# Attention heads in pairs on two tiles of TensorE, and a decay product with constant left sides

## The chip, the cores and the metric

The program runs on one core of one Trainium2 chip. The metric is the device time of one execution in microseconds (us); three runs of the kernel before took 1456.83 to 1459.18 us, with a median of 1458.25. Profiles are of one execution each, so a time read from a row is from that execution. Engine names: PE is TensorE (PEld its weight loads), DVE is VectorE, ACT is ScalarE, POOL is GpSimd, SP the engine that issues the loads here.

## The reference, cut to what matters

Two layers over 256 tokens of width 1024. Each layer has a mixer (attention, a short convolution and a gated recurrence, HGRN, side by side, from one input projection and into one output projection) and a channel mixer (dense SwiGLU in the first layer, eight experts with two chosen per token in the second). The change lies in the attention: 8 heads of 64, queries in two blocks of 128, logits shifted by the cumulated log of a forget gate.

```python
dcum = jnp.cumsum(jax.nn.log_sigmoid(f_logit.astype(jnp.float32)), axis=1)
...
logits = (jnp.einsum('bhqd,bhkd->bhqk', q_i, k_t) * scale
          + d_i[..., None] - d_k[:, :, None, :])
mask = k_pos[None, :] <= q_pos[:, None]
p = jax.nn.softmax(jnp.where(mask, logits, MASK_VALUE), axis=-1)
return jnp.einsum('bhqk,bhkd->bhqd', p, v_t)
```

A constant that is added to a whole row of logits (the term `d_i`) does not change its softmax.

## The kernel before

**Layout.** Activations stand transposed: features on the 128 partitions, the 256 tokens in the free dimension. Weights come in float32 in 1 MB pieces (`Stream`, lines 46 to 133): SP loads a piece into a `raw` buffer or into a large block `b0` to `b3` that has come free, ACT rounds it to a high part `whi` (line 107), DVE takes the rest as a low part `wlo` (line 117), and each projection is three matmuls: high x high, high x low, low x high. These have the output tile `z`, all in `mm` (line 362), and are most of what PE does.

**Order.** The tile framework schedules: it takes the order of the program text as a priority and writes out for each engine one fixed order of instructions, with waits between engines. On the chip every engine goes through its list in that order. The list `self.bg` holds pieces of background work; `tick` (line 165) issues the next one or more of them between groups of projection matmuls, so attention stands amid the projection of the convolution's inputs (`cxb`, `cc`, lines 685 and 689), and the output projection follows (`project`, line 714).

**Attention** (lines 456 to 684). `forget` (line 463) cumulates the gate on 104 partitions, four copies of eight heads at partitions 0, 32, 64 and 96, and splits it into a rounded and a remaining part: `dd` and `frhs`. `scores(n)` (line 629) makes a left side `lh` for head n on DVE (two columns of `h1`, `h2` select the head's rows), and then, for each of the two query blocks `t`, three matmuls into one PSUM bank of the tag `S`: `lh` x `frhs` (104 rows, 256 columns) gives the difference of the decays, `qn` x `kn` (64 rows, those of an even or an odd head; float32, which PE does in two passes) adds the logits, and `identb` x `causal` adds the mask. `attend(n)` (line 644) takes the maximum (DVE, line 651), the exponential with its sum (ACT, line 652), scales by the reciprocal (DVE, lines 653 and 655), turns three blocks of 128 x 128 on PE (line 659), copies them out (ACT, line 661, `pT`), multiplies by the values `av` into the even or odd half of a bank's partitions and copies that to `ya` (line 665). The background alternates `attend(n)` and `scores(n + 2)`. `hgrn_out` (line 561) and `out_norm` (line 572, tiles `on`, `E`, `rr`, `B`) stand between them. `over(i)` (line 671) hands a block to the stream of weights, in the second mixer for the experts. PSUM banks: three with the tag `z`, two `lv`, three `S` (line 151).

Of the kernel before, what the change touches and what calls it, by code (L numbers as in the profile page):

```python
# [18 lines left out]
T = 256  # L19
KT = D // P  # L20
# [19 lines left out]
SM_FB = 76  # L40
# [95 lines left out]
class Kern:  # L136
# [20 lines left out]

    def bank(self, tag="S"):

# [19 lines left out]
        parts.pop(0)()  # L179
        self.st.between = parts  # L180

    def constants(self, scr, itb):
# [3 lines left out]
        jp, it, ith = scr[:, 0:P], scr[:, P:2 * P].rearrange("p (k c) -> p k c", k=KT), scr[:104, 256:264]  # L186
# [13 lines left out]
        def later():  # L200
# [20 lines left out]
            for i in range(2):  # L221
                t = m.tile([48, T], F32R, name=f"rr{i}")
# [5 lines left out]
            nc.gpsimd.iota(ith, pattern=[[1, 8]], base=0, channel_multiplier=-1)  # L228
            self.h1 = m.tile([104, 8], F32, name="h1")
            self.h2 = m.tile([104, 8], F32, name="h2")  # L230
            self.ra = m.tile([104, 1], F32, name="ra")
            self.rb = m.tile([104, 1], F32, name="rb")
            for t in (self.h1, self.h2, self.ra, self.rb):
                nc.vector.memset(t, 0.0)
            for o in (0, 32, 64, 96):
                nc.vector.tensor_scalar((self.h2 if o < 64 else self.h1)[o:o + 8], ith[o:o + 8], float(-o), None,
                                        ALU.is_equal)
            nc.vector.memset(self.ra[0:8], -1.0)
            for o in (64, 96):
                nc.vector.memset(self.rb[o:o + 8], 1.0)  # L240
            self.ones104 = m.tile([104, T], F32, name="ones104")
            nc.gpsimd.memset(self.ones104, 1.0)

            self.reset = m.tile([P, 2, P], F32, name="reset")
            nc.gpsimd.memset(self.reset, 1.0)
# [3 lines left out]
            for w in (1, 2, 4, 8, 16, 32, 64):  # L249
                n = 64 // w  # L250
# [15 lines left out]
            sm = lbt[:, 2:4]  # L266
# [131 lines left out]
    def mixer_body(self, l, plan, h, hk, next_col, ta, tl, to, sml):  # L398
        nc = self.nc
# [7 lines left out]
        late = [self.constants(b2[:, 6 * T:8 * T], b3[0:16, 0:4 * T])] if l == 0 else []  # L407


        def forget_weights():  # L410
            wf = self.sm[:, SM_WF + 64 * l:SM_WF + 64 * (l + 1)].rearrange("p (k h) -> p k h", h=8)
            nc.gpsimd.memset(wp.bitcast(F32), 0.0)
            nc.gpsimd.memset(wq.bitcast(F32), 0.0)
            for o in (0, 32, 64, 96):
# [5 lines left out]
        R = rt = R2 = None  # L420
# [35 lines left out]
        dd = sml.tile([104, T], F32R, name="dd", bufs=1)  # L456
        rhs = sml.tile([104, T], F32R, name="frhs", bufs=1)
        fx = ta.tile([104, T], F32, name="fx", tag="t2")
        fa = ta.tile([104, T], F32, name="fa", tag="t2")
        fb = self.sm[:104, SM_FB + l:SM_FB + l + 1]  # L460
        nc.vector.tensor_tensor(fx, pf[:104], R[:104], ALU.mult)

        def forget():
            nc.scalar.activation(fa, fx, AF.Abs, bias=fb)
            nc.scalar.activation(fa, fa, AF.Exp, scale=-1.0)
            nc.scalar.activation(fa, fa, AF.Ln, bias=1.0)
            nc.vector.tensor_scalar(fx, fx, fb, 0.0, ALU.add, ALU.min)
            nc.vector.tensor_tensor(fx, fx, fa, ALU.subtract)


            nc.vector.tensor_tensor_scan(fa, self.ones104, fx, 0.0, ALU.mult, ALU.add)
            nc.scalar.activation(dd, fa, AF.Copy)
            nc.vector.tensor_scalar(rhs, dd.bitcast(F32), self.ra, self.rb, ALU.mult, ALU.add)
            nc.vector.tensor_tensor(rhs[32:40], dd[32:40].bitcast(F32), fa[32:40], ALU.subtract)
            nc.vector.tensor_tensor(dd[96:104], fa[96:104], dd[96:104].bitcast(F32), ALU.subtract)


        cum = part(b2, 4, 2)
# [117 lines left out]
        av = part(b3, 4, 4).rearrange("p (t a) c -> p t (a c)", t=2)  # L596
# [27 lines left out]


        ya = part(b3, 0, 4)
        S = {}

        def scores(n):
            if n > 7:  # L630
                return
            r, c = even_odd[n % 2], n // 2
            lh = sml.tile([104, T], F32R, name="lh", bufs=2)
            nc.vector.tensor_scalar(lh, dd.bitcast(F32), self.h1[:, n:n + 1], self.h2[:, n:n + 1], ALU.mult, ALU.add)
            b = self.bank()
            S[n] = (b[:, T:T + P], b[:, 0:T])
            for t in (1, 0):
                w = (t + 1) * P

                self.mm(b[:, (1 - t) * T:(2 - t) * T], lh[:, toks[t]], rhs, True, False)  # L640
                self.mm(S[n][t], qn[r, c, toks[t]], kn[r, c, 0:w], False, False)
                self.mm(S[n][t][:, w - P:w], self.identb, self.causal, False, True)

        def attend(n):
            r, c, vs = even_odd[n % 2], n // 2, slice(n * 64, n * 64 + 64)
            Pm = sml.tile([P, 3, P], F32, name="Pm", bufs=2)
            pm = (Pm[:, 2], Pm[:, 0:2].rearrange("p a b -> p (a b)"))
            nm = sml.tile([P, 2], F32, name="nm")
            sm = sml.tile([P, 2], F32, name="ssum")
            for t in (1, 0):  # L650
                nc.vector.tensor_reduce(nm[:, t:t + 1], S[n][t], AX.X, ALU.max, negate=True)
                nc.scalar.activation(pm[t], S[n][t], AF.Exp, bias=nm[:, t:t + 1], accum_out=sm[:, t:t + 1])
            nc.vector.reciprocal(sm, sm)
            for t in (1, 0):
                nc.vector.tensor_scalar(pm[t], pm[t], sm[:, t:t + 1], None, ALU.mult)

            pt = self.bank()
            for i, b in enumerate((2, 0, 1)):
                nc.tensor.transpose(pt[:, i * P:(i + 1) * P], Pm[:, b], self.ident)  # L659
            pT = sml.tile([P, 3 * P], F32, name="pT", bufs=2)  # L660
            nc.scalar.activation(pT, pt[:, 0:3 * P], AF.Copy)
            o = self.bank()[r, :T]
            self.mm(o, av[:, 0, vs], pT[:, 0:T], True, False)
            self.mm(o[:, P:T], av[:, 1, vs], pT[:, T:3 * P], False, True)
            nc.scalar.activation(ya[r, c], o, AF.Copy)

        scores(0)
        scores(1)


        def over(i):
# [1 line left out]
            if next_col is None:  # L673
                self.st.more(lambda: self.block(i))

        for n in range(8):
            self.bg += [lambda n=n: attend(n), lambda n=n: scores(n + 2)]
            if n == 1:
# [3 lines left out]
            if n == 5:  # L682
                self.bg.append(lambda: over(0))
        self.tick(2)
        z = self.chunk_t(plan["cxb"], h, 4, 3)
# [710 lines left out]
def layout(inputs):  # L1396

    import numpy as np
    g = {n: np.asarray(a) for n, a in inputs.items()}
    arrays = {n: np.ascontiguousarray(g[n]) for n in _WEIGHTS}  # L1400
    arrays["xt"] = np.ascontiguousarray(g["x"][0].T)

    def cols(a):
        return a.reshape(-1, a.shape[-1] // P, P).transpose(2, 0, 1).reshape(P, -1)

    def rows(a):
        return a.reshape(-1, KT, P, 8).transpose(2, 0, 1, 3).reshape(P, -1)

    fb = np.zeros((P, 2), g["attn_f_bias"].dtype)
    for o in (0, 32, 64, 96):  # L1410
# [24 lines left out]
```

## Time and profile before

| what | value |
|---|---|
| median of three runs | 1458.25 us (1456.83 to 1459.18) |
| profiled execution | 1458.15 us, span 1456.4 us |
| busy, share of the span | PE 97%, DVE 84%, ACT 71%, POOL 1% |
| mean granted clock | 0.992 |
| HBM read | 433.20 MB, 298 GB/s over the span |

The span is from the first to the last instruction; about 1.8 us of the execution lie around it. Matmuls are pipelined: a row's duration includes the time in which the next one already runs, so costs on PE are read from start to start, not from durations, and a busy PE is not one at its peak. A timeline row with x2 or x16 merges so many instructions that follow each other; its first number is the start of the first. The chain of work goes back from the last instruction to whatever released each step, so it names the engine that others wait for.

### The profile page before, as it was taken

The numbers are of one execution on the slowest core, as the hardware profiler recorded it, in microseconds if no ns is written. First come the engines' busy times: TensorE is split into PE (matmuls) and PEld (weight loads), VectorE is DVE, ScalarE is ACT, GpSimd is POOL, SyncE is SP. The second block draws the span as 40 slices with busy tenths as digits, with TensorE's granted clock in tenths as the row PEclk, the third lists the DMA queues.
The fourth block names the chain that finished last, engine by engine and source line by source line (L and its number), as shares of the span: only waits on it lengthen the run. The fifth ranks groups of instructions, "written<-read, shape, count | busy, mean of one in ns | idle before, by whom it ended". The sixth has DMA issues, their size and how long they took to land.

```text
span 1456.4 us, 21819 instructions
## 1 busy us (share of the span) xinstructions
PE 1415.0 (97%) x8339; PEld 1210.2 (83%) x8339; DVE 1229.3 (84%) x1257; ACT 1034.3 (71%) x1072; POOL 18.7 (1%) x39
## 2 busy tenths in 40 slices
PE   7999999999999998999999999999999999999997
PEld 7887999999999786788888778878888788877875
DVE  8957865555588677799989999998999999999997
ACT  8546643443474555789878788988888888888884
POOL 4000000000000000000000000000000000000000
PEclk9999999999999998999999999999999999999999
DMA  8332555555552356799999999999999999999994
GB/s 284 110 102 88 174 174 183 194 174 190 187 174 88 116 177 211 281 381 407 411 404 378 384 390 411 411 413 402 395 413 411 403 405 411 412 413 411 412 411 173
DMA packets 186766, 435.73 MB, mean 299 GB/s; under 512 B 6816, under 2 KB 11040, under 8 KB 186656
## 3 DMA queue, kind: packets, MB, share of 16 engines
q1 hardware_dynamic: 186656, 434.28, 79.3%
q8 instruction: 67, 1.10, 0.3%
q14 instruction: 43, 0.35, 0.1%
HBM read 433.20 MB, written 1.05 MB: 298 GB/s over the span
## 4 chain that ended last, share of the span: by engine, by line
PE 83%; DVE 8%; DMA 3%; issue 2%; ACT 2%; DVEq 0%; ACTq 0%
PE z L362 50%; PE S L362 14%; PE lv L362 10%; PE ls L362 7%; DVE wlo L117 5%; DMA b<-moe_w_gate 2%; DMA raw<-moe_w_up 1%; ACT whi L107 1%; PE S L1005 1%; DVE y L1042 1%; DVE xT L1051 0%; PE S L659 0%; DVE on L540 0%; DMA raw<-moe_w_down 0%; DVE b L556 0%
## 5 line engine op out<-in xcount | busy, mean ns | idle before, releaser
L117 DVE TENSOR_TENSOR wlo<-raw,whi 128x1024 fp32r<-128x1024 f32 (+2 forms) x287 | 479.3, 1683 | 95.7 <-issue 50.2
L107 ACT ACTIVATE whi<-raw 128x1024 fp32r<-128x1024 f32 (+2 forms) x287 | 405.1, 1427 | 164.3 <-PE z L362 93.0
L117 DVE TENSOR_TENSOR wlo<-b,whi 128x2048 fp32r<-128x2048 f32 (+1 forms) x177 | 395.4, 2247 | 11.4 <-PE z L362 4.0
L362 PE MATMUL z<-whi,x 128*128 128x512 f32 x1232 | 367.7, 402 | 3.2 <-DVE x L934 2.6
L107 ACT ACTIVATE whi<-b 128x2048 fp32r<-128x2048 f32 (+1 forms) x177 | 332.9, 1884 | 32.8 <-PE lv L362 7.5
L362 PE MATMUL z<-wlo,x 128*128 128x512 f32 x896 | 283.9, 398 | 3.5 <-DVE wlo L117 3.2
L362 PEld LDWEIGHTS z<-whi,x 128*128 128x128 f32 x1232 | 225.5, 190 | 50.3 <-DVE x L934 3.1
L362 PE MATMUL z<-hi,whi 128*128 128x256 f32 x864 | 246.5, 286 | 7.4 <-ACT whi L107 7.0
L362 PE MATMUL z<-lo,whi 128*128 128x256 f32 x864 | 245.6, 285 | 0.0
L362 PE MATMUL z<-hi,wlo 128*128 128x256 f32 x864 | 245.5, 285 | 0.0
L362 PEld LDWEIGHTS z<-wlo,x 128*128 128x128 f32 x896 | 167.9, 189 | 49.1 <-DVE wlo L117 9.1
L362 PEld LDWEIGHTS z<-hi,whi 128*128 128x128 f32 x864 | 164.2, 190 | 10.9 <-ACT whi L107 7.0
L362 PEld LDWEIGHTS z<-lo,whi 128*128 128x128 f32 x864 | 164.3, 190 | 1.6 <-issue 1.3
L362 PEld LDWEIGHTS z<-hi,wlo 128*128 128x128 f32 x864 | 163.9, 190 | 2.1 <-issue 0.8
L362 PE MATMUL ls<-whi,ah 128*128 128x512 f32 x264 | 83.8, 396 | 0.0
L362 PE MATMUL ls<-wlo,ah 128*128 128x512 f32 x264 | 83.7, 396 | 0.0
L362 PEld LDWEIGHTS ls<-wlo,ah 128*128 128x128 f32 x264 | 49.5, 188 | 12.2 <-DVE wlo L117 0.3
L362 PEld LDWEIGHTS ls<-whi,ah 128*128 128x128 f32 x264 | 49.3, 188 | 11.6
L117 DVE TENSOR_TENSOR wlo<-x,whi 128x2048 fp32r<-128x2048 f32 x24 | 54.6, 2284 | 3.7 <-PE z L362 3.4
L362 PE MATMUL lv<-whi,al 128*128 128x512 f32 x168 | 53.2, 395 | 0.0
L362 PE MATMUL lv<-wlo,ah 128*128 128x512 f32 x168 | 53.2, 395 | 0.0
L362 PE MATMUL lv<-whi,ah 128*128 128x512 f32 x168 | 53.2, 395 | 0.0
(336 smaller groups left out, 1765.8 us busy)
## 6 DMA issues: line engine op xcount, KB each, us to landing
b<-moe_w_gate SPq DMA_DIRECT2D x59, 1024.0 KB, 9.4
b<-moe_w_up SPq DMA_DIRECT2D x57, 1024.0 KB, 10.2
b<-moe_w_down SPq DMA_DIRECT2D x56, 1024.0 KB, 9.8
raw<-moe_w_up SPq DMA_DIRECT2D x45, 1024.0 KB, 10.2
raw<-moe_w_down SPq DMA_DIRECT2D x43, 1024.0 KB, 9.7
raw<-moe_w_gate SPq DMA_DIRECT2D x42, 1024.0 KB, 9.7
raw<-w_in SPq DMA_DIRECT2D x22, 1024.0 KB, 4.9
raw<-ffn_w_gate SPq DMA_DIRECT2D x14, 1024.0 KB, 5.0
```

The source lines that it names most:

```text
L107: self.nc.scalar.activation(hi, x, AF.Copy)
L117: self.nc.vector.tensor_tensor(lo, x, self.hi[i][:, h * a:(h + 1) * a].bitcast(F32), ALU.subtract)
L362: self.nc.tensor.matmul(out, lhsT, rhs, start=start, stop=stop, skip_group_check=True)
L1005: nc.tensor.transpose(pt[:, q * P:(q + 1) * P], a[0][:, q * P:(q + 1) * P], self.ident)
L1042: nc.vector.scalar_tensor_tensor(y2[:, 1, c], y[c], gs[:, 0:1], y2[:, 0, c].bitcast(F32), ALU.mult, ALU.subtract)
```

## The change

Heads are taken in pairs, an even one on partitions 0 to 63 and an odd one on 64 to 127.

- The decay product: `head`, a constant of 72 x 8 x 128 written once, selects a head's row (0 to 7: rounded part, 64 to 71: remaining part) for all 128 queries. `frhs` has 384 columns, minus the cumulated gate of all 256 tokens and again of the first 128, so one matmul per head serves both query blocks. The term `d_i` is left out. `dd`, `lh`, `h1`, `h2`, `ra` and `rb` go.
- `scores(p)`: both heads' decay products, then the four query-key products with the heads in turn (two row tiles, two banks), then the four masks; PE's order within this block is the written one.
- `attend(n)` becomes three pieces of background work: `soft(p)` (maximum to scaling, for two heads), `turn(p)` (six transposes, the second head's into a bank `lv`, two copies), and `attend(p)` (values of both heads into the two halves of one bank `lv`, heads in turn, one copy for both). Per pair the background is `soft(p)`, `scores(p + 1)`, `turn(p)`, `attend(p)`; before the first, only `scores(0)` is issued.

```diff
-        def scores(n):
-            if n > 7:
+        S, pms, pTs = {}, {}, {}
+
+        def scores(p):
+            if p > 3:
                 return
...
+            b = [self.bank(), self.bank()]
+            S[p] = [(x[:, T:T + P], x[:, 0:T]) for x in b]
+            with self.tc.manual_schedule(engines={mybir.EngineType.PE}):
+                for u in range(2):
+                    self.mm(b[u][:, 0:3 * P], self.head[:, 2 * p + u], rhs, True, False)
+                for t in (1, 0):
+                    for u, r in enumerate(even_odd):
+                        self.mm(S[p][u][t], qn[r, p, toks[t]], kn[r, p, 0:(t + 1) * P], False, False)
             for t in (1, 0):
...
+                for u in range(2):
+                    self.mm(S[p][u][t][:, t * P:(t + 1) * P], self.identb, self.causal, False, True)
...
+        def turn(p):
+
+            pTs[p] = sml.tile([P, 2, 3 * P], F32, name="pT", bufs=2)
+            for u in range(2):
+                pt = self.bank("lv" if u else "S")
+                for i, b in enumerate((2, 0, 1)):
+                    nc.tensor.transpose(pt[:, i * P:(i + 1) * P], pms[p][:, u, b], self.ident)
+                nc.scalar.activation(pTs[p][:, u], pt[:, 0:3 * P], AF.Copy)
+
+        def attend(p):
+            o = self.bank("lv")[:, :T]
+            for k in range(2):
+                for u, r in enumerate(even_odd):
+                    vs = slice((2 * p + u) * 64, (2 * p + u + 1) * 64)
+                    self.mm(o[r, k * P:T], av[:, k, vs], pTs[p][:, u, k * T:k * P + T], k == 0, k == 1)
+            nc.scalar.activation(ya[:, p], o, AF.Copy)
...
+            nc.gpsimd.iota(ith, pattern=[[1, 8], [0, P]], base=0, channel_multiplier=-1)
+            self.head = m.tile([72, 8, P], F32R, name="head")
+            for p, o in ((slice(0, 64), 0), (slice(64, 72), 64)):
+                nc.vector.tensor_scalar(self.head[p].rearrange("p n q -> p (n q)"),
+                                        ith[p].rearrange("p n q -> p (n q)"), float(-o), None, ALU.is_equal)
...
+            nc.vector.tensor_tensor_scan(fa, self.ones72, fx, 0.0, ALU.mult, ALU.add)
+            nc.scalar.activation(rhs[:, 0:T], fa, AF.Copy, scale=-1.0)
+            lo = rhs[64:72, 0:T]
+            nc.vector.scalar_tensor_tensor(lo, fa[64:72], -1.0, lo.bitcast(F32), ALU.mult, ALU.subtract)
+            nc.scalar.activation(rhs[:, T:3 * P], rhs[:, 0:P].bitcast(F32), AF.Copy)
...
+        for p in range(4):
+            self.bg += [lambda p=p, f=f: f(p) for f in (soft, lambda p: scores(p + 1), turn, attend)]
+            if p == 0:
                 self.bg.append(hgrn_out)
-            if n == 3:
+            if p == 1:
                 self.bg += [lambda: out_norm(6, yr), lambda: out_norm(0, ya[:, 0:2]), lambda: over(1)]
```

How the change moves instructions shows in the orders of the built programs. PE in the first mixer, before: the end of head 0's scores and the beginning of head 1's (each `S_` with its number is a bank's tile, `b0_686` holds queries and keys).

```order
L362 MATMUL S_1060<-b0_686 128x128
L362 LDWEIGHTS identb_298
L362 MATMUL S_1060<-causal_300,identb_298 128x128
L362 MATMUL S_1069<-frhs_557,lh_1067 128x256
L362 MATMUL S_1069<-b0_686 128x256
```

PE at the same place after the change: the scores of heads 0 and 1 (line numbers are those of the changed kernel; `S_1040` is the even head's bank, `S_1041` the odd one's).

```order
L356 MATMUL S_1041<-frhs_540,head_318 128x384
L356 MATMUL S_1040<-b0_669 128x256
L356 MATMUL S_1041<-b0_669 128x256
L356 MATMUL S_1040<-b0_669 128x128
L356 MATMUL S_1041<-b0_669 128x128
L356 LDWEIGHTS identb_294
L356 MATMUL S_1040<-causal_296,identb_294 128x128
```

Where one head's products of three kinds stood one after the other for each query block, the products of 64 rows now follow each other, the two heads in turn, and the masks come behind them. Between pair 0's masks and pair 1's products stand fifteen projection matmuls.

PE, before, from a head's transposes (`Pm`) to its value products (`pT`), first mixer, head 1.

```order
L659 MATMUL S_1145<-ident_147,Pm_1135 128x128 x3
L362 MATMUL z_1106<-hi_109,whi_872 128x256
L362 MATMUL z_1106<-lo_110,whi_872 128x256
L362 MATMUL z_1106<-hi_109,wlo_954 128x256
L362 MATMUL z_1106<-hi_113,whi_872 128x256
L362 MATMUL z_1106<-lo_114,whi_872 128x256
L362 MATMUL S_1151<-pT_1149,b3_139 64x256
L362 MATMUL S_1151<-pT_1149,b3_139 64x128
L362 MATMUL S_1157<-frhs_557,lh_1155 128x256
```

PE, after, from the transposes of pair 0 to its value products and what follows them (`lv_1133` is HGRN's output, `S_1191` pair 2's scores).

```order
L659 MATMUL S_1117<-ident_147,Pm_1055 128x128 x3
L659 MATMUL lv_1122<-ident_147,Pm_1055 128x128 x3
L356 MATMUL z_1086<-lo_122,whi_855 128x256
L356 MATMUL z_1086<-hi_121,wlo_937 128x256
L356 MATMUL lv_1127<-pT_1116,b3_139 64x256 x2
L356 MATMUL lv_1127<-pT_1116,b3_139 64x128 x2
L356 MATMUL lv_1133<-b2_138,b1_137 64x128 x12
L356 MATMUL S_1191<-frhs_540,head_318 128x384
```

Six transposes instead of three, then two projection matmuls instead of five, then the values of two heads; HGRN's output, which stood ahead of the attention, and the next pair's scores come behind.

SP, loads at the end of the second mixer's `w_out`, before: `b_5600` is block `b1`.

```order
L83 DMA raw<-w_out 128x2x1024 x3
L83 DMA b_5600<-w_out 128x2x1024
L83 DMA raw<-moe_w_gate 128x4x512 x2
L83 DMA b_5697<-moe_w_gate 128x4x512
L83 DMA raw<-moe_w_up 128x4x512
```

SP at the same place after the change.

```order
L83 DMA raw<-w_out 128x2x1024 x3
L83 DMA b_5600<-moe_w_gate 128x4x512
L83 DMA b_5513<-w_out 128x2x1024
L83 DMA raw<-moe_w_gate 128x4x512 x2
L83 DMA raw<-moe_w_up 128x4x512
```

The load of the first expert's gate weights into the block of queries and keys has moved ahead of the last quarter of `w_out`.

## Rows read from the trace of the kernel before

**Rows 1.** Chain of waits, 476 to 556 us, then 84 to 165: start us, us, what.
```profile
by line: PE z L362 46.3%; PE S L362 38.2%; PE lv L362 12.0%; PE S L659 3.5%; issue 0.1%
...
491.31 3.01 PE z L362 x25
...
by line: PE z L362 49.4%; PE S L362 37.6%; PE lv L362 7.9%; PE S L659 3.3%; ACT whi L107 1.3%; ACT hi L590 0.4%; issue 0.2%
...
99.25 4.53 PE z L362 x25
```
**Rows 2.** Stretches: us, then busy us of each engine, granted clock, DMA share, GB/s.
```profile
94.00:104.00 10.00, 10.00 (x58) 8.31 (x56) 6.68 (x18) 3.73 (x10) 0.00 (x0) 0.83 0.18 48
486.00:496.00 10.00, 10.00 (x64) 7.34 (x63) 7.28 (x19) 4.26 (x12) 0.00 (x0) 1.00 0.18 48
640.00:1000.00 360.00, 355.14 (x1706) 291.26 (x1705) 345.62 (x212) 306.01 (x236) 0.00 (x0) 1.00 1.03 402
```
**Rows 3.** Timeline of PE, scores of head 1: start us, us, engine, line, operation.
```profile
97.35 0.36 PE L362 MATMUL S<-frhs,lh 104*128 104x256 f32 x1
97.64 0.70 PE L362 MATMUL S<-b 64*128 64x256 f32 x2
98.27 0.23 PE L362 MATMUL S<-causal,identb 128*128 128x128 bf16 x1
98.31 0.36 PE L362 MATMUL S<-frhs,lh 104*128 104x256 f32 x1
98.60 0.48 PE L362 MATMUL S<-b 64*128 64x128 f32 x2
99.02 0.23 PE L362 MATMUL S<-causal,identb 128*128 128x128 bf16 x1
```
**Rows 4.** Timeline of PE, value products of head 0 and what follows.
```profile
105.13 0.86 PE L362 MATMUL S<-pT,b 128*64 128x256 f32 x4
105.92 0.38 PE L362 MATMUL S<-frhs,lh 104*128 104x256 f32 x1
```
**Rows 5.** Timeline of PE, HGRN's diagonal blocks (two row tiles) and what follows.
```profile
42.65 1.16 PE L362 MATMUL lv<-b 64*128 64x128 f32 x16
43.74 0.50 PE L362 MATMUL z<-whi,hi 128*128 128x512 f32 x1
```
**Rows 6.** Timeline of PE, HGRN's output (two column tiles) and what follows.
```profile
89.56 1.80 PE L362 MATMUL lv<-b,b 128*64 128x128 f32 x24
91.29 0.39 PE L362 MATMUL z<-hi,whi 128*128 128x256 f32 x1
```
**Rows 7.** Groups of ACT, 95 to 165 us: busy us, mean ns, idle before.
```profile
L661 ACT ACTIVATE pT<-S 128x384 f32<-128x384 f32 x8 | 3.9, 489 | 7.7 <-PE S L659 7.5
L652 ACT ACTIVATE Pm<-S,nm 128x256 f32<-128x256 f32 x8 | 3.8, 471 | 7.1 <-DVE nm L651 7.1
L652 ACT ACTIVATION_READ_ACCUMULATOR Pm<-S,nm 128x1 f32 x16 | 3.1, 197 | 0.0
...
L652 ACT ACTIVATE Pm<-S,nm 128x128 f32<-128x128 f32 x8 | 2.9, 361 | 0.8 <-DVE nm L651 0.7
```
**Rows 8.** Groups of DVE in the same stretch.
```profile
L651 DVE TENSOR_REDUCE nm<-S 128x1 f32<-128x256 f32 x8 | 3.4, 424 | 3.7 <-PE S L362 3.7
...
L655 DVE TENSOR_SCALAR Pm<-Pm,ssum 128x256 f32<-128x256 f32 x8 | 2.8, 347 | 0.1
L634 DVE TENSOR_SCALAR lh<-dd,h,h 104x256 fp32r<-104x256 f32 x6 | 2.5, 410 | 3.3 <-PE S L362 3.3
...
L655 DVE TENSOR_SCALAR Pm<-Pm,ssum 128x128 f32<-128x128 f32 x8 | 2.2, 278 | 0.0
...
L653 DVE RECIPROCAL ssum<-ssum 128x2 f32<-128x2 f32 x8 | 1.3, 157 | 0.9 <-ACT Pm L652 0.9
```
**Rows 9.** Group of DVE, 0 to 62 us: an operation of 1024 columns.
```profile
L218 DVE TENSOR_SCALAR B<-b 16x1024 fp32r<-16x1024 int32 x2 | 1.4, 679 | 0.0
```

More of the change, by code (lines that the diff above doesn't have):

```diff
@@ L180, in load_x, with constants @@
         self.st.between = parts
-    def constants(self, scr, itb):
+    def constants(self, scr, itb, ith):
         nc, c, m = self.nc, self.const, self.mconst
         scr, itb = scr.bitcast(I32), itb.bitcast(I32).rearrange("p (k a b) -> p k a b", k=KT, a=2)
-        jp, it, ith = scr[:, 0:P], scr[:, P:2 * P].rearrange("p (k c) -> p k c", k=KT), scr[:104, 256:264]
+        ith = ith.bitcast(I32).rearrange("p (n q) -> p n q", n=8)
+        jp, it = scr[:, 0:P], scr[:, P:2 * P].rearrange("p (k c) -> p k c", k=KT)
         onesf = scr.bitcast(F32)[:, 264:328]
@@ L226, in later @@
             nc.vector.tensor_scalar(self.gq8, self.sm[:, SM_GQ:SM_GQ + 2], 0.125, None, ALU.mult)
[L228 to L242, printed above, removed]
+            nc.gpsimd.iota(ith, pattern=[[1, 8], [0, P]], base=0, channel_multiplier=-1)
[3 more added lines that the diff above has]
+                                        ith[p].rearrange("p n q -> p (n q)"), float(-o), None, ALU.is_equal)
+            self.ones72 = m.tile([72, T], F32, name="ones72")
+            nc.gpsimd.memset(self.ones72, 1.0)
             self.reset = m.tile([P, 2, P], F32, name="reset")
@@ L406, in mixer_body @@
         b1, b2, b3 = (self.block(i) for i in (1, 2, 3))
-        late = [self.constants(b2[:, 6 * T:8 * T], b3[0:16, 0:4 * T])] if l == 0 else []
+        late = [self.constants(b2[:, 6 * T:8 * T], b3[0:16, 0:4 * T], b3[0:72, 4 * T:8 * T])] if l == 0 else []
         def forget_weights():
@@ L413, in forget_weights @@
             nc.gpsimd.memset(wq.bitcast(F32), 0.0)
-            for o in (0, 32, 64, 96):
+            for o in (0, 64):
                 nc.scalar.activation(wp[:, :, o:o + 8], wf, AF.Copy)
@@ L455, in mixer_body @@
             self.mm(pf, wq[:, k], h[k][0], False, k == KT - 1)
[L456 to L461, printed above, removed]
+        rhs = sml.tile([72, 3 * P], F32R, name="frhs", bufs=1)
+        fx = ta.tile([72, T], F32, name="fx", tag="t2")
+        fa = ta.tile([72, T], F32, name="fa", tag="t2")
+        fb = self.sm[:72, SM_FB + l:SM_FB + l + 1]
+        nc.vector.tensor_tensor(fx, pf[:72], R[:72], ALU.mult)
         def forget():
@@ L626, in mixer_body @@
         ya = part(b3, 0, 4)
-        S = {}
-        def scores(n):
-            if n > 7:
+        S, pms, pTs = {}, {}, {}
+        def scores(p):
+            if p > 3:
                 return
[L632 to L636, printed above, removed]
-            for t in (1, 0):
[L638 to L652, printed above, removed]
-            nc.vector.reciprocal(sm, sm)
[L654 to L665, printed above, removed]
@@ new lines, in soft @@
+        def soft(p):
+            Pm = sml.tile([P, 2, 3, P], F32, name="Pm", bufs=2)
+            nm = sml.tile([P, 2, 2], F32, name="nm")
+            sm = sml.tile([P, 2, 2], F32, name="ssum")
+            pms[p] = Pm
+            pm = [(Pm[:, u, 2], Pm[:, u, 0:2].rearrange("p a b -> p (a b)")) for u in range(2)]
+            for u in range(2):
+                for t in (1, 0):
+                    nc.vector.tensor_reduce(nm[:, u, t:t + 1], S[p][u][t], AX.X, ALU.max, negate=True)
+                    nc.scalar.activation(pm[u][t], S[p][u][t], AF.Exp, bias=nm[:, u, t:t + 1],
+                                         accum_out=sm[:, u, t:t + 1])
+            nc.vector.reciprocal(sm, sm)
+            for u in range(2):
+                for t in (1, 0):
+                    nc.vector.tensor_scalar(pm[u][t], pm[u][t], sm[:, u, t:t + 1], None, ALU.mult)
@@ new lines, in turn @@
+        def turn(p):
+            pTs[p] = sml.tile([P, 2, 3 * P], F32, name="pT", bufs=2)
+            for u in range(2):
+                pt = self.bank("lv" if u else "S")
[9 more added lines that the diff above has]
+            nc.scalar.activation(ya[:, p], o, AF.Copy)
@@ L667, in mixer_body @@
         scores(0)
-        scores(1)
         def over(i):
@@ L674, in over @@
                 self.st.more(lambda: self.block(i))
-        for n in range(8):
-            self.bg += [lambda n=n: attend(n), lambda n=n: scores(n + 2)]
-            if n == 1:
+        for p in range(4):
+            self.bg += [lambda p=p, f=f: f(p) for f in (soft, lambda p: scores(p + 1), turn, attend)]
+            if p == 0:
                 self.bg.append(hgrn_out)
-            if n == 3:
+            if p == 1:
                 self.bg += [lambda: out_norm(6, yr), lambda: out_norm(0, ya[:, 0:2]), lambda: over(1)]
-            if n == 5:
+            if p == 2:
                 self.bg.append(lambda: over(0))
@@ L1409, in layout @@
     fb = np.zeros((P, 2), g["attn_f_bias"].dtype)
-    for o in (0, 32, 64, 96):
+    for o in (0, 64):
         fb[o:o + 8] = g["attn_f_bias"].T
```

5 lines of the change are left out of this document (removed).

## The prediction

> **What bounds the kernel now.** I read the chain of work that ended last first, stretch by stretch, then the stretches with their granted clock, then TensorE's timeline inside the attention, then the groups of ScalarE and VectorE there. The attention runs twice, once in each mixer: at 95 to 141 us and at 488 to 533 us. In both stretches the reader is to see a chain that consists of TensorE and hardly anything else: 99% of 84 to 165 us and all but 0.1% of 476 to 556 us [rows 1]. TensorE does not wait there; so a microsecond less of its work is a microsecond less of the mixer, until another engine is late. Behind it the FFN stage and the expert stage follow; in the latter the DMA engines are full (share 1.03, 402 GB/s, row for 640 to 1000 us [rows 2]), and weights are loaded as buffers come free, so an earlier mixer starts that stream earlier.
>
> The second thing to see is the clock. In the first mixer the 25 projection matmuls behind two heads' scores took 4.53 us, in the second the same 25 took 3.01 us [rows 1]; the mean granted clock is 0.83 in 94 to 104 us and 1.00 in 486 to 496 us [rows 2]. So for some 3 us the array ran at the lower of its two levels, 1.2 instead of 2.4 GHz, after 3 us of nothing but scores; it cost 1.52 us in one mixer and nothing in the other.
>
> **What one head costs on TensorE before.** [Rows 3] hold one head's scores: 97.35 to 98.31 is 0.96 us for the later 128 queries (decay product 0.29, query-key product 0.63, mask 0.04), and from 98.31 another 0.29 + 0.42 + 0.04 = 0.75 for the earlier ones: 1.71 us a head, 3.42 a pair. Of each 0.29 only 0.12 is streaming (3.01 us / 25 for the same 256 columns [rows 1]); the rest, 0.17, is the change from the full array to a tile of 64 rows, which a head pays twice, and about as much is paid on the way back. The value products take 105.13 to 105.92, 0.79 us a head, 1.58 a pair [rows 4].
>
> **The change, part by part.**
>
> Scores. A pair now has two decay products of 384 columns (384/256 x 0.12 = 0.18 each, 0.36), one change of array shape (0.17), the query-key products of both heads on two row tiles in turn, and four masks in a row. Two row tiles in turn stand in the trace already: the diagonal blocks of the HGRN part, 16 passes of 128 columns in 42.65 to 43.74 [rows 5], 1.09 us, so 0.14 for a pair of passes with both changes of shape in it. One head has four passes, 0.63 + 0.42 less the changes in the middle (about 0.2) = 0.85; if the tiles overlap as in rows 5, the pair takes that 0.85. Masks: from below 0.04 each [rows 3], from above 0.12, a whole projection matmul of twice the columns [rows 1]; I take 0.3 for the four, near the middle, since each loads its left side anew and not in the shadow of a change of shape. Sum 0.36 + 0.17 + 0.85 + 0.3 = 1.68 against 3.42: 1.74 us saved a pair (1.56 to 1.88 by the bounds of the masks).
>
> Values. Two heads go to two column tiles of one bank. The trace shows that too: HGRN's output, 24 passes of 128 columns in 89.56 to 91.29 [rows 6], 0.072 each, where the passes of a single tile can't do better than (0.79 - 0.2)/6, about 0.10 per 128 columns [rows 4]. So a pair takes about one head's 0.79: 0.79 saved.
>
> Together 2.53 us a pair, 8 pairs: 20.2 us. The transposes are as many as before.
>
> New waits. In the order, two projection matmuls (0.24 us) now stand between a pair's six transposes and its value products, where five stood before and only three transposes (one copy). ScalarE has to copy both heads' probabilities, 0.49 us each, one after the other [rows 7]; the second is done about 0.5 us after TensorE wants it. Behind the waiting product stand, on TensorE, HGRN's output and the next pair's scores, and behind those everything else. I put 0.5 us at pairs 0 and 1, 0.3 at 2 and 3, 1.6 a mixer. Softmax: from a pair's last mask to its scaled rows it takes 0.42 (a maximum) + 2 x (0.47 + 0.20) + 2 x (0.36 + 0.20) (the exponentials with their sums) + 0.16 + 2 x 0.35 + 2 x 0.28 (the scaling) = 4.3 us [rows 7, 8]. The cover in the order: for pair 0, fifteen projection matmuls (1.8) and pair 1's scores (1.7); for pair 1, values of pair 0, HGRN's output (1.73) and scores of pair 2; for pairs 2 and 3 over 20 projection matmuls. So it is hidden but for about 0.4. Waits: 2 us a mixer, 4 us in all; bounds 0 (copies hidden) and 8 (twice that).
>
> The clock. The stretch from pair 1's scores to pair 1's values now holds almost no projection matmuls, some 9 us where before it was 3 (the one that cost 1.52). Packed tiles do more work per microsecond, the waits less. From below the loss of 1.52 goes away (gain 1.5), from above two such losses in each mixer (6.1, so 4.6 more than before). I take one in each mixer, the nearest row: 1.5 us more than now.
>
> Small parts. The 16 products of `lh` leave VectorE, 0.41 us each [rows 8], and half of the copies and reciprocals leave too: VectorE and ScalarE are not on the chain there, so nothing. The constant left sides add two VectorE operations of 1024 columns (0.68 each [rows 9]) and take away small ones there; taken as if VectorE stood on the chain then, that is 0.3 us (bounds 0 and 1.4). The decay's second half is copied once on ScalarE, hidden behind the key scaling. The load of the last quarter of `w_out` goes behind one of `moe_w_gate` on SP's queue and so behind the release of another buffer, that of the queries and keys, which the last pair's scores give free; it is used only after the last value product, the last heads' norm and three quarters of the output projection: hidden. If that load were late, its landing would be the next thing waited for.
>
> Sum: 20.2 - 4 - 1.5 - 0.3 = 14.4 us. The profiled execution took 1458.15 us with what lies around its span, 0.1 below the median of the three runs. 1458.15 - 14.4 = 1443.75: **1444 us**.
>
> The Trainium skill, TensorEngine Tiling (Array Packing), section PSUM Bottleneck, speaks against this change: tiling makes TensorE faster but not the copies out of PSUM, which may then become the bound. By rows a pair costs ScalarE 2 x 0.47 + 2 x 0.36 + 2 x 0.49 us and four sum reads, 3.4 in all [rows 7], while the stretch of 46 us (95 to 141) gives a pair 11.5, or 9 after the saving: by averages the copies do not bind, where two matmuls alone stand between transposes and values they do, which is the 1.6 above; by the rule alone it would be the last rival below.
>
> **Rivals.**
> (a) The expert stage doesn't profit from the second mixer: its DMA engines are full [rows 2], and if its first loads wait for something other than the mixer, half of the gain is lost: 1458.15 - 7.2 = 1451. For it: the full engines later. Against: a DMA share of 0.18 at 486 to 496 us [rows 2] and loads into buffers that the mixer frees.
> (b) No loss at the lower clock and the copies hidden: 20.2 + 1.5 - 0.3 = 21.4, 1437. For it: the second mixer's clock of 1.00; against: the two matmuls between.
> (c) The tiles don't overlap, so that the change does not do what it says: a pair's query-key passes one after the other are about 1.5, scores 2.33, values 1.58: 1.09 saved a pair, 8.7, less 1.5, 0.3 and some 2 of waits: 1453. Against it rows 5 and 6.
> (d) Slower: TensorE's order puts a pair's transposes behind too little, and it waits for the softmax. If only the next pair's scores covered it, 4.3 - 1.7 + 1.0 (copies) = 3.6 us a pair would be open, 28.8 in all: 1458.15 - 20.2 + 28.8 + 1.8 = 1468. It decides from 2.3 us of waits a pair ((20.2 - 1.8)/8). For it: VectorE and ScalarE take their work in order, among the weight splits. Against: the order shows the cover named above.
>
> **How the numbers follow.** Forecast 0.53, (a) 0.15, (b) 0.12, (c) 0.06, (d) 0.08; 0.06 that lesser losses add up to no change. About 0.2%, 2.9 us, is what a measurement can tell from none. Faster: 0.53 + 0.15 + 0.12 + 0.06 = 0.86; same 0.06; slower 0.08. The forecast's own range is 1439 to 1449 (waits and clock between their bounds); with (a) and (b) and part of (c) it is 1437 to 1453.
>
> **What would show it.** In the profile after: scores of a pair in about 1.7 us and values in 0.8 between their first and the next matmul's start; starts of two heads' passes a few ns apart; TensorE idle before value products until ScalarE's copy, about 0.5 us, twice to four times a mixer; a granted clock below 1 in some 3 us of each attention; the second mixer's end some 14 us earlier, and the same difference at the end of the span. The prediction is wrong if passes of the two tiles start one behind the other, if TensorE waits over 2 us a pair, or if the expert stage ends less early than it begins.

## The result and the profile after

The changed kernel took 1440.12 us (median of 4 runs, 1439.78 to 1441.26) beside 1458.72 us for the kernel before: 18.6 us less, a ratio of 0.9874 (95% interval 0.9857 to 0.9891). 1444 was forecast. Its profiled execution took 1441.26 us, with a span of 1439.5, so 1.1 us above its median; the stages below are from that span, which is 16.8 us shorter than that of the kernel before.

The chain of waits of the second mixer, 476 to 540 us, answers to [rows 1]:

```profile
by line: PE z L356 42.9%; PE lv L356 22.4%; PE S L356 19.2%; PE lv L659 2.5%; PE S L659 2.1%; DVE wlo L117 1.8%; DVE Pm L651 1.6%; DVE rr L368 1.3%; DVE t L690 0.9%; issue 0.7%; ACT rs_t L279 0.7%; DVE frhs L467 0.7%; ACT rr L367 0.7%; DVE 
```

TensorE was all but 0.1% of it; now its lines make 89%, and short stretches of VectorE and ScalarE (softmax, norms, a weight split) stand between them. TensorE itself is idle for more than 0.1 us only once in that mixer. The stretches of [rows 2] in the kernel after (us, busy us of PE, PEld, DVE, ACT and POOL, granted clock, DMA share, GB/s):

```profile
94.00:104.00 10.00, 9.99 (x94) 8.49 (x93) 7.30 (x19) 6.71 (x21) 0.00 (x0) 1.00 0.31 105
480.00:490.00 10.00, 9.99 (x94) 8.41 (x94) 7.24 (x22) 6.55 (x22) 0.00 (x0) 1.00 0.30 107
640.00:1000.00 360.00, 354.67 (x1719) 291.18 (x1718) 343.01 (x215) 305.54 (x249) 0.00 (x0) 1.00 1.03 401
```

The clock is 1.00 in both attentions (also over all of 95 to 140 and of 474 to 540 us), and the expert stage has the same full DMA engines. The scores of one pair, on PE, answer to [rows 3]; then the value products of pair 1 and those of pair 2, to [rows 4]:

```profile
104.11 0.62 PE L356 MATMUL S<-frhs,head 72*128 72x384 f32 x2
104.66 0.92 PE L356 MATMUL S<-b 64*128 64x256 f32 x8
105.51 0.40 PE L356 MATMUL S<-causal,identb 128*128 128x128 bf16 x4
105.75 0.28 PE L659 MATMUL S<-ident,Pm 128*128 128x128 f32 x1
...
106.83 1.25 PE L356 MATMUL lv<-pT,b 128*64 128x256 f32 x8
108.00 1.04 PE L356 MATMUL lv<-on,E 128*16 128x256 f32 x4
...
125.27 0.87 PE L356 MATMUL lv<-pT,b 128*64 128x256 f32 x8
126.07 0.33 PE L659 MATMUL lv<-ident,Pm 128*128 128x128 f32 x1
```

From 104.11 to 105.75 two heads' scores take 1.64 us, where two heads took 3.42; in the single instructions the second head's first pass starts 6 ns after the first head's. From 125.27 to 126.07 two heads' values take 0.80, where one took 0.79. From 106.83 to 108.00 they take 1.17, for pair 1 has to wait for its second copy; pairs 0 and 3 wait too, pair 2 does not.

To see where the time went I cut the span at six instructions that every kernel has: the first product of the query norms in each mixer, the first sum into the residual `xT` at the end of the first mixer, of the FFN and of the second mixer, the same for the first expert block, and one late in the expert stage. Lengths in us:

| stage | before | after | difference |
|---|---|---|---|
| start to the first query norm | 69.28 | 69.59 | +0.31 |
| to the end of mixer 1 | 90.98 | 82.47 | -8.51 |
| FFN | 240.60 | 242.01 | +1.41 |
| to the second query norm | 60.48 | 60.62 | +0.14 |
| to the end of mixer 2 | 88.26 | 78.54 | -9.72 |
| routing, to the first expert's sum | 256.86 | 254.95 | -1.91 |
| to a sum near 1110 us | 322.28 | 322.21 | -0.07 |
| rest | 327.62 | 329.13 | +1.51 |

The mixers gave 18.2. The last two rows and the first wander by 1.6 to 2.5 us among the kernels below (68.7 to 70.9, 321.9 to 323.5, 327.0 to 329.5), whatever is changed; the others repeat to about 0.2 where neither their work nor the clock differs. Inside the second mixer, TensorE's time from the start of one product to the start of the next, added up by kind, before and after: decay products 4.65 and 2.07, query-key products 8.37 and 3.42, masks 0.67 and 0.88, transposes 2.00 and 2.26, value products 6.35 and 4.16, projections (all of `z`) 47.66 and 47.10.

### The profile page after: what moved, and what is told of

Same layout as the page of the kernel before. It is cut to its first block, busy times and chain, and to the rows that moved or that the text cites. A ratio compares the mean times of both kernels' runs of the same rounds, so it can differ in the third digit from the quotient of the medians.

```text
span 1439.5 us, 21728 instructions
## 1 busy us (share of the span) xinstructions
PE 1393.2 (97%) x8323; PEld 1200.9 (83%) x8323; DVE 1221.7 (85%) x1216; ACT 1029.7 (72%) x1062; POOL 19.6 (1%) x39
## 4 chain that ended last, share of the span: by engine, by line
PE 81%; DVE 10%; DMA 3%; ACT 2%; issue 2%; DVEq 0%; ACTq 0%
PE z L356 49%; PE S L356 12%; PE lv L356 11%; PE ls L356 7%; DVE wlo L117 5%; DMA b<-moe_w_gate 3%; ACT whi L107 1%; PE S L1007 1%; DVE y L1044 1%; DVE xT L1053 0%; DVE b L549 0%; DVE on L533 0%; PE lv L659 0%; PE S L659 0%; DVE al L1019 0%
```

## The experiments

Unless said otherwise, stage lengths are those of the table, "mixer 1" and "mixer 2" its rows 2 and 5; edits are shown abridged. Stages are of one profiled execution, totals medians of four or more.

**e1_const_left: one part alone.** The kernel before with the constant left sides, heads one by one.

```
-  for t: mm(b[..], lh[:, toks[t]], rhs); mm(S[n][t], qn, kn); mask
+  mm(b[:, 0:3*P], head[:, n], rhs)
+  for t: mm(S[n][t], qn, kn)
+  for t: mask
```

> The kernel before with one part of the change alone: the decay product of a head is one product of 384 columns from the constant left side; heads stay one by one, with their value products and copies as before. Theory 1 (the terms are additive and each sits where the sum put it): per mixer the 16 decay products of 4.66 us become 8 of about 2.1, the two query-key products of a head lose the change of shape between them (8.37 to about 6.8), the masks rise by 0.2: 4.0 us a mixer, 8.0 in all, less 0.45 for the longer constants: about 1451 beside 1458.7. Theory 2 (the gain is the pairing; the left sides alone only save streaming, 0.06 us a head): at most 1 us, 1457.5 or more.

1454.66 us, 0.9979 (0.9969 to 0.9988) of the kernel before, between the theories. One head's scores in its PE timeline:

```profile
106.06 0.44 PE L356 MATMUL S<-frhs,head 72*128 72x384 f32 x1
106.42 0.92 PE L356 MATMUL S<-b 64*128 64x256 f32 x4
107.27 0.28 PE L356 MATMUL S<-causal,identb 128*128 128x128 bf16 x2
```

The query-key products of one head take 0.85 us (106.42 to 107.27), 6.79 a mixer, as the sum had it. The decay products take 2.75, not 2.1: alone, each takes 0.36 us to the first product of 64 rows (106.06 to 106.42), where a pair's two take 0.55 (104.11 to 104.66). Mixer 2 lost 2.78, so the left sides by themselves give 2.8 of its 9.7 and the pairing 6.9. Mixer 1 lost only 1.23, for a new wait of 1.85 us at its end, and the FFN took 242.03 here too.

**e2_rows_apart and e3_cols_apart: does the turn matter?**

```
-  for t in (1, 0):            # query-key products
-      for u in heads: mm(S[p][u][t], ...)
+  for u in heads:
+      for t in (1, 0): mm(S[p][u][t], ...)
```

> The changed kernel with one loop turned: a pair's four query-key products run head by head (same row tile twice, then the other), not in turn; nothing else moves. Theory 1 (the two row tiles overlap only when neighbours alternate): a pair's query-key part goes from 0.855 us to about 1.5 (two heads of 0.85 less one shared change of shape), 8 pairs: +5.2, about 1445.3. Theory 2 (the drop from 8.37 to 3.42 us a mixer is fewer changes of shape, not overlap, or neighbours overlap at the one border anyway): +0.5 or less, 1440.5.

1439.47 us (0.9873, 0.9858 to 0.9888): no change. The same pair in it:

```profile
103.97 0.93 PE L356 MATMUL S<-b 64*128 64x256 f32 x8
104.83 0.40 PE L356 MATMUL S<-causal,identb 128*128 128x128 bf16 x4
```

0.86 us for eight passes, as in turn (0.85). In the single instructions its second head's first pass starts 14 ns after the first head's, though by the program's order two passes of the first head's other block stand ahead of it. So neighbours on two row tiles overlap in either order.

e3 turns the same two loops in the value products.

> The changed kernel with one loop turned: a pair's value products run head by head, not in turn on the two column tiles. Theory 1 (the second head's copy of probabilities is late at pairs 0, 1 and 3, so that the tiles in turn do not overlap there, and head by head the first head works while the copy runs): only pair 2 of each mixer loses the whole overlap, 0.58 us, the others 0.1 each: +1.8, about 1442. Theory 2 (the overlap is worth its full 0.58 us at every pair): +4.6, about 1444.7.

1437.99 us (0.9868, 0.9853 to 0.9883): neither theory. Value products of 4.12 us in mixer 2 against 4.16: column tiles overlap in either order too, and nothing was lost. Mixer 2 is 0.24 shorter; mixer 1 is 1.50 shorter for another reason (the clock, below).

**e7_heads_split: is it overlap at all?** The second head's decay product, a product over the full array, put between the heads.

```
-  for u: mm(decay u)
-  for t: for u: mm(S[p][u][t], ...)
+  for u: mm(decay u); for t: mm(S[p][u][t], ...)
```

> The changed kernel with the second head's decay product put between the two heads' query-key products, so that a full-array product parts the two row tiles. Theory 1 (the pair's 0.855 us is two heads side by side, 0.85 each alone): query-key products 3.42 to 6.8 us a mixer and the decay products 2.08 to 2.75, 4.05 a mixer, 8.1 in all: about 1448. Theory 2 (only changes of array shape were saved, 0.17 each, two a pair): +2.7, about 1443.

1444.78 us (0.9901, 0.9880 to 0.9922). PE, one pair:

```profile
482.25 0.92 PE L356 MATMUL S<-b 64*128 64x256 f32 x4
483.09 0.44 PE L356 MATMUL S<-frhs,head 72*128 72x384 f32 x1
483.46 0.92 PE L356 MATMUL S<-b 64*128 64x256 f32 x4
484.31 0.40 PE L356 MATMUL S<-causal,identb 128*128 128x128 bf16 x4
```

Each head again has 0.84 to 0.85 us of its own. Query-key products rose from 3.42 to 6.67 us, decay products from 2.07 to 2.55, mixer 2 from 78.54 to 81.71. Theory 1 has the mechanism, with 3.2 of its 4.05 in mixer 2; the total rose by 4.7, not 8.1, since in mixer 1 the wait at the end went at the same time (82.88 there, with no idle stretch).

**e8_copy_dve: the copies.** The second head's probabilities are copied by VectorE.

```
-  nc.scalar.activation(pTs[p][:, u], pt[:, 0:3 * P], AF.Copy)
+  if u: nc.vector.tensor_copy(pTs[p][:, u], pt[:, 0:3 * P])
+  else: nc.scalar.activation(...)
```

> The changed kernel with the second head's copy of its probabilities on VectorE instead of ScalarE. Theory 1 (the value products wait for two copies of 0.49 us, one behind the other on ScalarE: by the trace 0.27 inside and 0.09 ahead of them at pairs 0, 1 and 3): 1 us a mixer goes, second mixer 78.5 to 77.6 us from its first query norm to its end, total about 1438. Theory 2 (VectorE's own queue, softmax of the next pair and weight splits of 1.22 us, makes that copy later still): 0 to 2 us more, 1440 to 1442.

1444.27 us (0.9904, 0.9885 to 0.9923): 4 us slower than the changed kernel, mixer 2 80.56 against 78.54, mixer 1 83.14 against 82.47, the routing 1.25 more, and in all more than Theory 2 gave. What the copies do in the changed kernel, pair 0, PE and ScalarE:

```profile
100.88 0.49 PE L659 MATMUL lv<-ident,Pm 128*128 128x128 f32 x3
101.08 0.49 ACT L660 ACTIVATE pT<-S 128x384 f32<-128x384 f32 x1 [1.59 <-PE S L659]
101.34 0.28 PE L356 MATMUL z<-hi,wlo 128*128 128x256 f32 x1
101.47 0.48 ACT L660 ACTIVATE pT<-lv 128x384 f32<-128x384 f32 x1
101.63 1.03 PE L356 MATMUL lv<-pT,b 128*64 128x256 f32 x6
```

and VectorE's copies in e8, 455 to 536 us (busy us, mean ns, idle before):

```profile
L661 DVE COPY pT<-lv 128x384 f32<-128x384 f32 x4 | 2.2, 553 | 1.1 <-PE lv L659 1.1
```

The second head's last transpose starts at 101.10 and ends at 101.37, and ScalarE starts its copy at 101.47: one engine for both copies costs 0.1 us, not 0.4. VectorE's copy is longer (553 ns against 489 of [rows 7]), and the order that the scheduler then wrote puts the next decay product or two projections between the heads' value products, which rose from 4.16 to 4.99 us. The Trainium skill, TensorEngine Tiling (Array Packing), section PSUM Bottleneck, advises both engines for such copies; here that cost 2.7 us in the two mixers and 4 in all. How much of it is the longer copy and how much the other order was not parted.

**e4_norm_first: the wait at the end of mixer 1.** PE, DVE and ACT of the changed kernel there:

```profile
138.08 2.00 ACT L107 ACTIVATE whi<-raw 128x1024 fp32r<-128x1024 f32 x2 [0.36 <-PE S L356]
138.20 1.23 DVE L117 TENSOR_TENSOR wlo<-raw,whi 128x1024 fp32r<-128x1024 f32 x1
138.32 0.47 PE L356 MATMUL lv<-rr,B 48*128 48x256 f32 x2 [0.15 <-DVE rr L368]
139.34 0.87 DVE L580 SCALAR_TENSOR_TENSOR on<-b,sm,lv 128x256 f32<-128x256 f32 x2
139.99 0.40 ACT L583 ACTIVATE hi<-on 128x256 fp32r<-128x256 f32 x1
140.44 0.62 PE L356 MATMUL z<-hi,whi 128*128 128x256 f32 x3 [1.65 <-ACT hi L583]
```

TensorE stands from 138.79 to 140.44. It waits for ScalarE's copy `hi` of the convolution's norm, and ahead of that stand a weight split on VectorE (1.23, which delays the norm's last product `on`) and two on ScalarE (2.00). The kernel before waited 0.37 at this place. The attention's last columns had been ready since 128.5.

```
-  out_norm(4, yc); over(2); out_norm(2, ya[:, 2:4]); over(3)
+  out_norm(2, ya[:, 2:4]); over(3); out_norm(4, yc); over(2)
```

> The changed kernel with the last two groups of heads' norms exchanged: the attention's columns 2 and 3, ready first now, before the convolution's 4 and 5, and the rows of w_out in that order. Theory 1 (what the change gave back at the first mixer's end is the 1.65 us in which TensorE waits for the copy of the convolution's norm behind two weight splits of ScalarE, and the 1.5 us that 15 matmuls then lose at the lower clock): both go, about 1437. Theory 2 (the norm that is now last has the same chain of some 7 us and is late in its turn): 1440 as before.

1438.85 us (0.9863, 0.9848 to 0.9878). Mixer 1 went from 82.47 to 79.06, 3.4 us as Theory 1 had it, with no idle stretch. The medians differ by 1.3 only; in its profiled execution the first query norm came 1.15 later and the routing took 0.8 more, both among the stages that wander. So the 3.4 us are shown for the stage, not for the total.

Behind this wait the clock fell. The changed kernel's chain behind the wait, its stretches there, and the same stretches of e3:

```profile
142.40 3.25 PE z L356 x15
```

```profile
140.00:143.00 3.00, 2.56 (x11) 1.51 (x12) 2.02 (x4) 1.76 (x6) 0.00 (x0) 0.80 0.15 18
143.00:146.00 3.00, 3.00 (x19) 3.00 (x19) 1.65 (x4) 0.76 (x2) 0.00 (x0) 0.64 0.91 334
```

```profile
140.00:143.00 3.00, 3.00 (x19) 2.21 (x20) 1.88 (x4) 1.63 (x4) 0.00 (x0) 1.00 0.33 61
143.00:146.00 3.00, 3.00 (x24) 2.73 (x23) 1.75 (x6) 0.42 (x1) 0.00 (x0) 1.00 0.77 290
```

The idle stretch is 1.65 and 1.66 us. In the one the granted clock fell to 0.64 and 15 matmuls took 3.25 us, in the other it stayed at 1.00: that is e3's 1.50. Of five executions with this wait (changed kernel twice, e2, e3, e5) four lost it. Two more had a longer one at this place: e1 (1.85) lost it too, e8 (1.86) kept 1.00. The changed kernel lost it both times, and e3 and e8 have another order of instructions, so whether chance or order decides is not shown.

**e5_gap128 and e6_before_gap: the FFN's 1.4 us.** The FFN has the same instructions before and after, and TensorE is never idle in it. The new constants had moved its operands by 3968 bytes. e5 adds 128 dead bytes to the changed kernel, e6 3968 to the kernel before:

```
+  nc.gpsimd.memset(m.tile([P, 32], F32, name="gap"), 0.0)     # e5
+  nc.gpsimd.memset(m.tile([P, 992], F32, name="gap"), 0.0)    # e6
```

> The changed kernel with one dead constant of 128 bytes a partition behind the constants, which puts the operands hi, lo, ah, al of the later stages exactly 4096 bytes behind their places in the kernel before (now it is 3968). The FFN stage, with the same instructions as before and TensorE never idle, took 240.60 us in the kernel before and 242.01 to 242.07 in all five kernels with the new constants. Theory 1 (the places of the operands set the 1 to 2 ns by which a projection product is longer): FFN back to 240.6, total 1.5 us less, about 1438.6. Theory 2 (something else, say the weights' landing times): 242.0 stays.

> The kernel before with a dead constant of 3968 bytes a partition, which puts its operands where the changed kernel has them. Theory 1 (places): FFN 242.0 instead of 240.6, total +1.5 beside the kernel before. Theory 2: 240.6. Beside it, the way from the second mixer's end to the first expert's end took 256.9 us in the kernel before, with a granted clock of 0.62 in 5 us of it, and 255.0 in the others with a clock of 1.00 there: if that clock was one execution's chance, 255 appears here too; if it is tied to the time at which the old attention ends, 256.9.

The two sums that begin and end the FFN, on DVE, in the kernel before, after, e5 and e6:

```profile
160.26 0.68 DVE L732 TENSOR_TENSOR xT<-xT,z 128x512 f32<-128x512 f32 x1
...
400.86 0.68 DVE L732 TENSOR_TENSOR xT<-xT,S 128x512 f32<-128x512 f32 x1
```

```profile
152.06 0.68 DVE L734 TENSOR_TENSOR xT<-xT,z 128x512 f32<-128x512 f32 x1
...
394.07 0.68 DVE L734 TENSOR_TENSOR xT<-xT,S 128x512 f32<-128x512 f32 x1
```

```profile
151.50 0.68 DVE L734 TENSOR_TENSOR xT<-xT,z 128x512 f32<-128x512 f32 x1
...
392.04 0.68 DVE L734 TENSOR_TENSOR xT<-xT,S 128x512 f32<-128x512 f32 x1
```

```profile
159.33 0.68 DVE L732 TENSOR_TENSOR xT<-xT,z 128x512 f32<-128x512 f32 x1
...
401.40 0.68 DVE L732 TENSOR_TENSOR xT<-xT,S 128x512 f32<-128x512 f32 x1
```

240.60 before, 242.01 after, 240.54 and 242.07: Theory 1 in both directions. TensorE goes through the same products in the same order in all four. By the means from start to start, products on `hi` and `lo` are 0.6 to 2.1 ns longer after than before and those on `ah` and `al` 0.9 to 1.5 ns shorter; with e5's gap all are back within 0.1. So the places cost 1.4 us; that it is those of TensorE's own operands, and not of something else that moved with them, is likely by this but not shown. e6 took 1460.7 us (1.0017, 1.0007 to 1.0027), e5 1439.93 (0.9868, 0.9849 to 0.9888): the changed kernel's time, 1.3 above Theory 1; in its profiled execution the routing took 256.90 instead of 254.95. The time of that stage goes with the clock. Two parts of the routing, and then all of it, before and after:

```profile
566.40:571.60 5.20, 5.20 (x19) 4.44 (x20) 4.72 (x22) 5.20 (x4) 0.00 (x0) 0.62 0.55 192
577.20:582.50 5.30, 5.30 (x16) 4.32 (x17) 4.18 (x11) 0.60 (x2) 0.00 (x0) 0.50 1.03 400
...
549.60:806.46 256.86, 248.08 (x1205) 202.70 (x1203) 231.23 (x202) 207.96 (x189) 0.24 (x1) 0.97 0.94 355
```

```profile
550.00:555.20 5.20, 3.60 (x20) 2.77 (x18) 4.67 (x23) 5.20 (x5) 0.00 (x0) 1.00 0.59 202
560.80:566.10 5.30, 5.30 (x21) 4.41 (x20) 4.63 (x11) 1.91 (x2) 0.00 (x0) 0.68 1.03 401
...
533.23:788.18 254.95, 244.09 (x1205) 199.42 (x1203) 231.18 (x201) 207.94 (x189) 0.25 (x1) 0.99 0.95 358
```

Over all of it the clock was 0.97 in the kernel before, e5 and e10 and 0.98 in e6 (256.7 to 256.9 us), 0.99 in the ten others (255.0 to 256.2). Old and new attention, old and new places are on the slower side, so the 1.9 us of the first table are not put down to the change; what sets it stays open. And e6 has the old attention with another clock:

```profile
94.00:104.00 10.00, 10.00 (x64) 7.39 (x64) 7.28 (x19) 4.21 (x11) 0.00 (x0) 1.00 0.15 44
486.00:496.00 10.00, 10.00 (x66) 7.80 (x65) 7.28 (x18) 3.99 (x11) 0.00 (x0) 1.00 0.10 10
```

1.00 in both, as over the whole of its mixer 1, where [rows 2] have 0.83 in the first.

**e9 to e12: put together, and once more.** e9 is e4 with e5's gap; e10 adds HGRN's output between transposes and value products of pair 0, the sums of HGRN's norm between those of pair 1, and e3's order; e11 is e9 with 32 dead bytes; e12 is the changed kernel again.

```
-  [soft, scores(p+1), turn, attend]; p == 0: hgrn_out; p == 1: out_norm(6)      # e10
+  [soft, scores(p+1), turn]; p == 0: hgrn_out; p == 1: out_norm(6); attend
```

> Two things found here put together on the changed kernel: the attention's last norm ahead of the convolution's (first mixer 82.5 to 79.1 us) and the 128 dead bytes that put the operands back in step (FFN 242.0 to 240.5, mixers 0.3 less each). Theory 1 (the gains add): 3.4 + 1.5 + 0.6 = 5.5 less than the changed kernel where the clock plays no part, about 1435. Theory 2 (what comes before the routing is given back there by the clock, which fell in it in some kernels and cost 1.9): 1437.

> The kernel of the run before with the waits at the value products covered too: HGRN's output between the transposes and the value products of pair 0, the HGRN norm's sums between those of pair 1, and the value products head by head. Theory 1 (the waits that are left, 0.36 us at pairs 0, 1 and 3 of each mixer, go for pairs 0 and 1): 0.7 a mixer less, second mixer 78.2 to 77.5, total about 1.4 less than the run before. Theory 2 (ScalarE's order makes another instruction late, as with the copy on VectorE): no gain, or up to 2 us more.

> As the run before last, with 32 dead bytes instead of 128. No theory gives a figure: 128 bytes restore the old places modulo 4096. If only places modulo 64 bytes count, hi and lo are then on a multiple of 64 (the old and the changed kernel both have 32 over), and FFN is neither 240.5 nor 242.0; if it is places modulo 128 or more, it may be either.

> The changed kernel once more, beside the others on the same chip. Theory 1 (the losses at the lower clock are a matter of the single execution): the 1.5 us after the first mixer's wait, or the figure for the way to the first expert's end (254.95), may differ, all other stages agree within 0.1 us (mixers 82.5 or 81.0 and 78.5, FFN 242.0). Theory 2 (the clock follows from the order of the work): the same figures within 0.1.

| | median us | ratio to before | mixer 1 | FFN | mixer 2 | routing |
|---|---|---|---|---|---|---|
| e9 | 1436.10 | 0.9852 (0.9838 to 0.9865) | 78.78 | 240.60 | 78.20 | 254.98 |
| e10 | 1434.27 | 0.9841 (0.9826 to 0.9856) | 78.42 | 240.40 | 77.18 | 256.71 |
| e11 | 1434.93 | 0.9847 (0.9832 to 0.9862) | 78.90 | 239.40 | 78.28 | 255.77 |
| e12 | 1440.35 | 0.9888 (0.9870 to 0.9907) | 82.52 | 242.01 | 78.56 | 255.33 |

The gains add stage by stage (e9's 1436.1 lies between its two theories), and e10 took 0.4 us less than e9 in mixer 1 and 1.0 in mixer 2. Its value products fell from 4.16 to 3.68 in mixer 2, but its transposes rose from 2.26 to 2.51, so most of the 1.0 lies in projections and HGRN's output and is not shown to be waits. 32 bytes are better still in the FFN. That it is then neither 240.5 nor 242.0 fits a rule of places modulo 64 bytes, but one more place does not show it. By their medians e9, e10 and e11 are below both kernels; e10's order with e11's gap was not run. e12 repeats the changed kernel's mixers and FFN within 0.05, loss of clock included, as Theory 2 has it; its routing differs by 0.4, as Theory 1 allows.

## Why the prediction was right, and where it was not

- **Scores: right.** 1.74 us a pair was taken, within 1.56 to 1.88; TensorE's sums by kind give (4.65 + 8.37 + 0.67 - 2.07 - 3.42 - 0.88) / 4 = 1.83; the masks, taken at 0.3, took 0.22. The mechanism, a pair's products in one head's time, is shown by e1 and e7. That the products must stand in turn is not: e2.
- **Values: right.** 0.80 us for pair 2, the one without a wait, where one head's 0.79 was taken.
- **Waits: half the size.** 2 us a mixer were taken. Value products beyond 4 x 0.80 are 0.96 us in mixer 2 (4.16 - 3.20), with about 0.1 ahead of three of them: 1.2. They stand at pairs 0, 1 and 3; pair 2 has none, where 0.3 was taken. Other work in front of them takes the value products of pairs 0 and 1 to 0.80 (e10). Its reason, two copies in a row on ScalarE, holds for 0.1 us each; the rest is transposing and copying as such, by the rows of pair 0 above. No wait for the softmax.
- **Clock: the wrong term.** One loss in each mixer was taken, from the one loss in [rows 2]. There was none in either attention, and e6 shows the old attention, with its operands at other places, without it: one execution's event was priced as a fixed cost of that stretch. The term was 1.5 us lost and became 1.5 gained.
- **Not foreseen: the end of mixer 1.** With the attention over at 128 us, the convolution's norm was late, and the clock fell behind the wait: 3.4 us there, by e4. The prediction asked what was next late at the value products and the softmax, not at the norm behind them. Mixer 1 still gave 8.5, for the kernel before had a loss of clock of its own in it.
- **Not foreseen: the FFN's 1.4 us**, by e5 and e6. The costs of the constants were looked for on VectorE, where they are as priced ([rows 9] against the two new operations below), and not in where they push the rest.
- **The number: near in part by luck.** 14.4 us were forecast, and the mixers gave 18.2. Scores gave 0.7 more than was taken, value products less their waits and transposes 1.6 more, the clock in the attention 3.0 more; against that stand the 3.4 at the end of mixer 1, which no term had. Some 1.6 more are spread over other products and 0.3 was taken for constants that lie outside the mixers. Outside the mixers the FFN took 1.4 more and the last row 1.5 more, and the routing, with the clock, 1.9 less.
- **Two slips.** The range of 1439 to 1449 is narrower than its bounds: with waits and clock both at theirs it is 1437 to 1451. The measured 1440.12 lies in both. TensorE's lines in the second chain of [rows 1] add up to 98.2%, not 99%; nothing hangs on that.
- **Rivals.** (a) fell: the second mixer ended 16.4 us earlier (549.60 to 533.23), the first expert's sum 18.3. The span ended 16.8 earlier, 1.5 less than that sum, which by the prediction's last sign would speak against it; but the 1.5 stand in the table's last row, which wanders by 2.5, so they decide nothing. (c) fell by e7. (d) fell: 0.3 us of waits a pair, not 2.3. (b), 1437, had the clock right and the copies wrong. The load of `w_out` moved behind one of `moe_w_gate` was hidden: the only idle stretch of TensorE over 0.1 us in mixer 2 is 0.17, for a norm.

The constants on VectorE, 0 to 62 us, after:

```profile
L233 DVE TENSOR_SCALAR head<-b 8x1024 fp32r<-8x1024 int32 x1 | 0.7, 684 | 0.0
L233 DVE TENSOR_SCALAR head<-b 64x1024 fp32r<-64x1024 int32 x1 | 0.7, 678 | 0.0
```

## What to carry to other kernels

Price two tiles by one head alone (0.85) and by a pair already in the trace, and keep full-array products out from between them; the order inside the pair can be left. When a stage gets shorter, follow each chain that used to end beside it, and see who now stands ahead of its small copies on VectorE and ScalarE. A drop of the granted clock seen in one execution is a range, not a term; and where a constant changes size, compare a stage that the change does not touch.

## What the runs showed of the hardware

- Products on two tiles start 6 to 14 ns apart in either order of the program, as long as nothing over the full array stands between (changed kernel, e2, e3); with such a product between, the second tile's first one starts 1.2 us later (e7). This agrees with the Trainium skill, TensorEngine Tiling (Array Packing), section Key Properties, that tiles operate independently.
- Where the tiles behind the constants lie in SBUF, TensorE's operands among them, changes TensorE's pace: with the same FFN instructions 242.0 us, 240.5 with 128 bytes more (e5) and 239.4 with 32 bytes more (e11). Which part of the address counts was not settled.
- After nearly the same idle stretch (1.64 to 1.66 us) the granted clock fell in four executions (0.64 in 3 us of the changed kernel) and stayed at 1.00 in a fifth (e3); behind 1.85 us it fell in e1, behind 1.86 it stayed in e8.
